# Output projection of a conformer-attention encoder: weights re-cut from four 256-column to two 512-column blocks, with a new, fully pinned order

## The chip, the cores and the metric

One NeuronCore of a Trainium2 chip. The core has five engines that run their own queues in order: PE (TensorE, matrix products into PSUM; its weight loads are shown as PEld), DVE (VectorE), ACT (ScalarE), POOL (GpSimd) and SP (SyncE, which issues the DMAs here). The metric is the device time of one execution in microseconds (us), as the median of several runs. Verdicts are about this time alone.

## What is computed

Two sequences of 512 tokens (a prompt and a sample), each with 16 meta tokens in front, go through one encoder layer. Width is 1024, everything is float32. Cut to what matters here:

```
hn = rms(h) ; z = hn @ w_in                       # gate, value, latent q, latent kv, rope key
u  = silu(layernorm(depthwise_conv(c_val * sigmoid(c_gate))))   # 512 channels
o  = attention(q, k, v)                           # 8 heads x 64 = 512 columns
h  = h + concat([u, o]) @ w_out                   # the output projection, 1024 x 1024
h  = h + (silu(rms(h) @ w_gate) * (rms(h) @ w_up)) @ w_down
return rms(h)[:, 16:]
```

The change concerns the line with `w_out`, the layer norm and silu of the convolution that feed it, and the order in which these stand beside the attention's end and the FFN's beginning.

## The kernel before

**Numbers.** Every product of float32 matrices is made of three matmuls in a reduced format: each operand is split into a high part (a cast, on ACT) and a low part (the remainder, a subtraction on DVE or POOL), and `mm3` (L160) multiplies high by high, high by low and low by high into the same PSUM place. A weight tile of 128 x 1024 floats is loaded and split by `pair` (L143): a DMA to a `raw` tile (two of them), a cast on ACT (L149), a subtraction on POOL (L152), into one of four `pair` tiles.

**PSUM.** There are four one-bank places (`bank`, tile `pt`) and two two-bank places (`bank2`, tile `ps`; the FFN's transposes use them as `px`).

**The output projection.** The K dimension of 1024 has two halves: half 0 is the convolution branch (`u`), half 1 the attention branch (`o`), each four tiles of 128 rows. The output's 1024 columns are cut in four blocks `dq` of 256, the tokens in eight tiles `t` of 128 (t = 0 to 3 the first sequence, 4 to 7 the second). `w_out_block(half, dq, t)` (L988) is 12 matmuls, each 128 tokens x 256 columns, and one DVE addition of the PSUM place onto the residual tile `hres[t]` (L994). `hres[0]` to `hres[2]` are tiles of their own; `hres[3]` to `hres[7]` lie in `slots`, where the attention had put its output `o`; x is loaded into them (L986) once that has been split. A weight tile `wo[2 * dq + half]` holds four k tiles by 256 columns.

**Half 1 and the layer norm.** Token tile 0 of half 1 is multiplied early, as a filler in the attention's last head (`early_blocks`, L864). The rest runs in the loop at L1006: `dq` from 0 to 3, `t` from 1 to 7, and at given positions (`steps`, numbered dq * 8 + t) stand the layer norm of a token tile (`layer_norm`, L946: four transposes into a two-bank place, statistics on DVE, two small POOL operations, one DVE operation, one ACT operation into one of two `xs` tiles), the way back (`layer_back`, L968: four transposes, one ACT copy into `U`) and the silu with its split (`conv_silu`, L975: two ACT operations, one DVE). The first layer norm stands at position 2, each further one 2 later, the way back 4 after it. After each `dq` the half-0 weight pair of that `dq` is loaded.

**Who sets the order.** Without more, the framework's planner orders the instructions of each engine by priority and its own time estimate. An instruction passed through `pin` (L125) while `pinned[0]` is true is kept behind everything that the program has issued to that engine before it. In the kernel before, `pinned[0]` becomes true only after the half-1 loop, at L1241, and the operations of layer norm, way back, silu and weight split aren't passed through `pin` at all.

**Half 0 and the FFN's beginning.** The list in `run` (L1276) is a hand-written order: tuples `(dq, t)` are half-0 blocks; `sq(t)` is the sum of squares of a finished token tile (ACT, then two POOL operations, L192 to L194; it also writes the tile to DRAM); `sc(t)` scales it (two DVE operations, L1045); `tu(t, s)` transposes eight 128 x 128 tiles on PE into a two-bank place (L1060); `do(t, stages)` splits tokens t and t + 4 and their sums and differences (the FFN uses Strassen-like combinations; L1064 to L1101); `co(j)` makes the weight operands of FFN unit 0 (L1136 to L1154), and the second list adds `pr(j)`, that unit's products over tokens 0 to 255.

## Time and profile before

| | |
|---|---|
| median of 3 runs | 1099.79 us (1099.77 to 1099.86) |
| the profiled execution | 1100.08 us; span of its instructions 1098.3 us |
| granted TensorE clock | 0.999 |
| DVE, ACT, POOL busy | 829.0, 497.5, 475.9 us |
| half-0 and half-1 matmuls of the projection from the loop's tiles | 128 x 256 |
| matmuls of the FFN | 128 x 512 for the most part |

The profile is one execution seen by the hardware profiler. A row of a timeline gives the start in us from the span's start, the duration, engine, line, operation, and output tile <- input tiles with shapes; a bracket at its end gives the idle time ahead of it and who ended it. A duration of a matmul is modelled and overlaps the next one's, so the distance between starts is what one costs. `x2` after a row means two instructions merged into it. A row of the windows gives, for each engine, the busy time inside the stretch and the number of instructions. The chain of waits is followed back from the last instruction: at each step to what released it.

### The profile page before, as it was taken

What the parts mean: (1) busy time and instruction counts of PE and PEld (TensorE: products, weight loads), DVE (VectorE), ACT (ScalarE), POOL (GpSimd) and SP (SyncE); (2) the same over time, 40 slices, a digit from 0 to 9 for tenths busy, and PEclk for the clock granted to TensorE, in tenths of its full rate; (3) what the DMA queues carried; (4) which work ended last, traced back from release to release, by engine and by line L of the source; (5) the groups of instructions that cost most, each with busy time, mean ns of one, the idle gap of its engine ahead of it and who ended that gap; (6) DMA issues with size and microseconds to landing.
All of it is one profiled execution on the core that took longest, in us unless ns stands there. A gap on an engine that the chain in (4) does not pass through costs nothing.

```text
span 1098.3 us, 16027 instructions
## 1 busy us (share of the span) xinstructions
PE 1075.8 (98%) x5922; PEld 929.5 (85%) x5922; DVE 829.0 (75%) x1206; ACT 497.5 (45%) x836; POOL 475.9 (43%) x419
## 2 busy tenths in 40 slices
PE   8999999999999999899999999999999999999997
PEld 8989888888888999788888888888888888888886
DVE  5699997888887646999877876877687496656643
ACT  6554525787786534542223233322322355433331
POOL 4689735564563233775544554554555200000012
PEclk9999999999999999999999999999999999999999
DMA  7211111110100412245445426444543899865503
GB/s 295 78 39 44 44 39 61 39 55 4 40 22 35 157 58 97 77 148 186 130 160 192 169 94 207 164 140 148 201 157 103 298 329 338 293 197 182 182 22 133
DMA packets 71422, 147.08 MB, mean 134 GB/s; under 512 B 6944, under 2 KB 29728, under 8 KB 71344
## 3 DMA queue, kind: packets, MB, share of 16 engines
q1 hardware_dynamic: 71344, 146.06, 38.9%
q8 instruction: 47, 0.77, 0.3%
q14 instruction: 31, 0.25, 0.1%
HBM read 105.92 MB, written 40.11 MB: 133 GB/s over the span
## 4 chain that ended last, share of the span: by engine, by line
PE 56%; DVE 2%; issue 2%; DMA 0%; POOL 0%; ACT 0%; POOLq 0%; ACTq 0%; SPq 0%; DVEq 0%
PE pt L167 48%; PE ps L167 8%; DMA raw<-in_w_gate_dram 0%; DVE tt L1045 0%; DVE hf L1045 0%; DVE tt L1136 0%; DVE slots L994 0%; DVE act_l L1067 0%; POOL rs L194 0%; DVE h L1087 0%; POOL slots L1442 0%; DVE slots L1086 0%; DVE slots L1094 0%; DVE a12l L1067 0%; DVE h L1091 0%
## 5 line engine op out<-in xcount | busy, mean ns | idle before, releaser
L167 PE MATMUL pt<-act_h,wc 128*128 128x512 f32 (+1 forms) x552 | 175.1, 380 | 0.0
L1154 POOL TENSOR_TENSOR wc<-tt,wc 128x512 fp32r<-128x512 f32 x88 | 124.6, 1432 | 104.4 <-ACT wc L1152 60.2
L167 PEld LDWEIGHTS pt<-act_h,wc 128*128 128x128 f32 x552 | 102.5, 188 | 19.6
L193 POOL TENSOR_SCALAR ms<-ms 128x1 f32<-128x1 f32 x15 | 7.3, 485 | 242.6 <-ACT re L192 214.1
L167 PE MATMUL pt<-hn_h,wp 128*128 128x512 f32 (+2 forms) x448 | 107.0, 331 | 0.0
L167 PE MATMUL pt<-act_l,wc 128*128 128x512 f32 (+1 forms) x276 | 104.8, 380 | 0.0
L1152 ACT CAST wc<-tt 128x512 fp32r<-128x512 f32 x88 | 51.4, 617 | 116.5 <-PE pt L167 109.8
L1334 DVE TENSOR_TENSOR re<-re,re 128x1024 fp32r<-128x1024 f32 x53 | 64.1, 1223 | 45.9 <-ACT re L1333 45.8
L1333 ACT CAST re<-re 128x1024 fp32r<-128x1024 f32 x53 | 55.0, 1054 | 69.2 <-PE ps L167 20.0
L167 PE MATMUL pt<-re 128*128 128x512 f32 x360 | 84.0, 389 | 0.0
L167 PEld LDWEIGHTS pt<-hn_h,wp 128*128 128x128 f32 x448 | 75.8, 188 | 8.5
L167 PEld LDWEIGHTS pt<-re 128*128 128x128 f32 x360 | 67.6, 188 | 14.0
L152 POOL TENSOR_TENSOR wp<-raw,wp 128x1024 fp32r<-128x1024 f32 x24 | 58.5, 2439 | 40.5 <-ACT wp L149 40.5
L167 PE MATMUL pt<-hn_l,wp 128*128 128x512 f32 (+2 forms) x224 | 74.5, 332 | 0.0
L742 POOL TENSOR_SCALAR p<-p,sst 128x512 f32<-128x512 f32 x64 | 44.1, 696 | 65.3 <-DVE sst L740 57.4
L167 PE MATMUL pt<-wp,act_h 128*128 128x256 f32 x384 | 71.2, 285 | 0.0
L1154 POOL TENSOR_TENSOR wc<-raw,wc 128x512 fp32r<-128x512 f32 x33 | 45.5, 1390 | 52.1 <-ACT wc L1152 52.1
L167 PE MATMUL ps<-re 128*128 128x512 f32 x276 | 63.9, 389 | 0.0
L367 POOL TENSOR_TENSOR pacc<-pacc,prod 128x512 f32<-128x512 f32 x43 | 58.3, 1355 | 7.0 <-ACT prod L365 4.3
L167 PEld LDWEIGHTS ps<-re 128*128 128x128 f32 x276 | 51.8, 188 | 10.7
L167 PEld LDWEIGHTS pt<-act_l,wc 128*128 128x128 f32 x276 | 51.9, 188 | 9.8
L167 PEld LDWEIGHTS pt<-wp,act_h 128*128 128x128 f32 x384 | 59.9, 192 | 0.2
(296 smaller groups left out, 2937.5 us busy)
## 6 DMA issues: line engine op xcount, KB each, us to landing
raw<-in_w_gate_dram SPq DMA_DIRECT2D x22, 512.0 KB, 3.9
hf<-in_w_down_dram SPq DMA_DIRECT2D x44, 256.0 KB, 4.8
re<-in_w_down_dram SPq DMA_DIRECT2D x31, 256.0 KB, 5.3
raw<-in_w_in_dram SPq DMA_DIRECT2D x12, 512.0 KB, 3.6
slots<-in_w_up_dram SPq DMA_DIRECT2D x11, 512.0 KB, 3.5
h<-in_w_up_dram SPq DMA_DIRECT2D x11, 512.0 KB, 5.5
d_t1t<-hf SPq DMA_DIRECT2D x22, 256.0 KB, 5.4
d_t4t<-hf SPq DMA_DIRECT2D x22, 256.0 KB, 2.5
```

What stands on the lines that cost most here:

```text
L152: nc.gpsimd.tensor_sub(lo[:, a], raw[:, a], hi[:, a].bitcast(F32))
L167: pin(nc.tensor.matmul(out_ap, lhsT=w_, rhs=m_, start=first and i + j == 0, stop=last and i == n - 1 and j == 2))
L193: pin(nc.gpsimd.tensor_scalar(ms[:rows], ms[:rows], EPS, 0.0, op0=ALU.add, op1=ALU.add))
L367: nc.gpsimd.tensor_add(acc, acc, to)
L742: nc.gpsimd.tensor_scalar(pr[:, real], pr[:, real], st[:, 2, t:t + 1], 1.0, op0=ALU.mult, op1=ALU.mult)
L1152: pin(nc.scalar.copy(w[:, 0:512], src))
L1154: pin(lo_eng.tensor_sub(w[:, 512:1024], src, w[:, 0:512].bitcast(F32)))
L1333: nc.scalar.copy(w[:, :, LO], blocks[n])
L1334: nc.vector.tensor_sub(w[:, :, HI], blocks[n], w[:, :, LO].bitcast(F32))
```

## The change

1. The projection's weights are packed as two k tiles by 512 columns per 128 x 1024 tile, eight tiles as before: `wo[4 * e + 2 * half + k // 2]` holds k tiles k and k + 1 of column half `e`. `wo_cut` picks a k tile's 512 columns.
2. `w_out_block(half, e, t)` makes 12 matmuls of 128 x 512 and one addition of 128 x 512. There are 16 half-0 blocks where there were 32, and 14 in the half-1 loop where there were 28. The early filler has as many steps (8), each of 3 matmuls of 512 columns in place of 6 of 256.
3. `pinned[0]` becomes true before the half-1 loop, and layer norm, way back, silu, the early addition and the casts and subtractions of `pair` are passed through `pin`. DMAs are not.
4. Positions: block (e, t) stands at e * 16 + 2 * t and is followed by the steps of that and the next position. Layer norm i stands at 6 + 2 * i, the way back at 10 + 2 * i, the silus of sequence s at 20 + 6 * s + c. Token tile 0 has no block in the loop, but its positions' steps stay.
5. The weight pairs of half 0's first column half (wo[0], wo[1]) are made after blocks (1, 4) and (1, 5) of the half-1 loop; those of the second (wo[4], wo[5]) inside the half-0 list (`ld`), as is the load of the first FFN weights.
6. The half-0 list has a new order.

```diff
@@ -49,7 +49,7 @@
 POOL_TAPS = (12, 13, 10, 12)
 LATE_TAPS = 0
 WARM = (36, 4, 8)
-LN_FIRST = 2
+LN_FIRST = 6
 LN_BACK = 4
 LN_STEP = 2
 SILU_STEP = 2
@@ -77,6 +77,7 @@
 ORDER_DOWN = (0, 1, 2, 4, 3, 6, 5)
 LOAD_AT = 5
 WO_AT = (4, 6)
+WO_CONV_AT = (4, 5)
 MM = "h"
 SC = "w"
 PV = False
@@ -146,10 +147,10 @@
         raw = raw_load(src)
         both = pool.tile([P, 2, 1024], F32R, tag=tag, bufs=bufs, name=name("wp"))
         hi, lo = both[:, 0, :], both[:, 1, :]
-        nc.scalar.copy(hi, raw)
+        pin(nc.scalar.copy(hi, raw))
         for a in range(0, 1024, LO_W):
             a = slice(a, a + LO_W)
-            nc.gpsimd.tensor_sub(lo[:, a], raw[:, a], hi[:, a].bitcast(F32))
+            pin(nc.gpsimd.tensor_sub(lo[:, a], raw[:, a], hi[:, a].bitcast(F32)))
         return hi, lo
 
     def split(hi, lo, src, pin=False):
@@ -861,18 +862,20 @@
         split(to[0][:, :, cs], to[1][:, :, cs], o[:, :, s * SEQ + t * 128:s * SEQ + (t + 1) * 128],
               pin)
 
+    def wo_cut(e, half, k):
+
+        return tuple(wx[:, k % 2 * 512:(k % 2 + 1) * 512] for wx in wo[4 * e + 2 * half + k // 2])
+
     def early_blocks():
 
         for t in range(EARLY):
-            for dq in range(4):
-                if dq == 0:
+            for e in range(2):
+                if e == 0:
                     early.append(bank2())
-                out_ap = early[t][:, dq // 2, dq % 2 * 256:(dq % 2 + 1) * 256]
                 cs = slice(t * 128, (t + 1) * 128)
-                for k0 in (0, 2):
-                    mm3(out_ap, [(o_first[0][:, k, cs], o_first[1][:, k, cs]) for k in (k0, k0 + 1)],
-                        [tuple(wx[:, k * 256:(k + 1) * 256] for wx in wo[2 * dq + 1]) for k in (k0, k0 + 1)],
-                        first=k0 == 0, last=k0 == 2)
+                for k in range(4):
+                    mm3(early[t][:, e, :], [(o_first[0][:, k, cs], o_first[1][:, k, cs])], [wo_cut(e, 1, k)],
+                        first=k == 0, last=k == 3)
                     yield
 
     filler = early_blocks()
@@ -880,7 +883,7 @@
         if s == 0 and h == LOAD_AT:
             wvp = load_attn(1)
         if s == 1 and h in WO_AT:
-            for n in (4 * WO_AT.index(h) + 1, 4 * WO_AT.index(h) + 3):
+            for n in (4 * WO_AT.index(h) + 2, 4 * WO_AT.index(h) + 3):
                 wo[n] = pair(w_out[n])
         nxt = heads[i + 1] if i + 1 < len(heads) else None
         if nxt is not None:
@@ -950,19 +953,19 @@
         pt = bank((P, 4, 128)) if LN_T else bank2()[:, 0].rearrange("p (c n) -> p c n", c=4)
         for c in range(NCH):
             src = late[:, s] if c == NCH - 1 else U[:, c, s]
-            nc.tensor.transpose(pt[:, c, :], src[:, ts], ident)
+            pin(nc.tensor.transpose(pt[:, c, :], src[:, ts], ident))
         st = const.tile([P, 6], F32, tag="bst", bufs=2, name=name("bst"))
         ag = const.tile([P, 2], F32, tag="bag", bufs=2, name=name("bag"))
         rs = const.tile([P, 1], F32, tag="brs", bufs=2, name=name("brs"))
         nm = const.tile([P, 1], F32, tag="bnm", bufs=2, name=name("bnm"))
         flat = pt.rearrange("p c n -> p (c n)")
-        nc.vector.bn_stats(st, flat)
-        nc.vector.bn_aggr(ag, st)
-        nc.gpsimd.tensor_scalar(rs, ag[:, 1:2], EPS, 0.0, op0=ALU.add, op1=ALU.add)
-        nc.gpsimd.tensor_tensor(rs, rs, mhalf[:, 0:1], op=ALU.pow)
-        nc.vector.scalar_tensor_tensor(nm, ag[:, 0:1], -1.0, rs, ALU.mult, ALU.mult)
+        pin(nc.vector.bn_stats(st, flat))
+        pin(nc.vector.bn_aggr(ag, st))
+        pin(nc.gpsimd.tensor_scalar(rs, ag[:, 1:2], EPS, 0.0, op0=ALU.add, op1=ALU.add))
+        pin(nc.gpsimd.tensor_tensor(rs, rs, mhalf[:, 0:1], op=ALU.pow))
+        pin(nc.vector.scalar_tensor_tensor(nm, ag[:, 0:1], -1.0, rs, ALU.mult, ALU.mult))
         xs = normed[i] = lnp.tile([P, SEQ], F32, tag="xs", bufs=XS, name=name("xs"))
-        nc.scalar.activation(xs, flat, AF.Identity, scale=rs, bias=nm)
+        pin(nc.scalar.activation(xs, flat, AF.Identity, scale=rs, bias=nm))
 
     def layer_back(i):
         s, t = divmod(i, 4)
@@ -970,28 +973,27 @@
         xs = normed[i]
         pt = bank((P, 4, 128)) if LB_T else bank2()[:, 0].rearrange("p (c n) -> p c n", c=4)
         for c in range(NCH):
-            nc.tensor.transpose(pt[:, c, :], xs[:, c * 128:(c + 1) * 128], ident)
-        nc.scalar.copy(U[:, :, s, ts], pt)
+            pin(nc.tensor.transpose(pt[:, c, :], xs[:, c * 128:(c + 1) * 128], ident))
+        pin(nc.scalar.copy(U[:, :, s, ts], pt))
 
     def conv_silu(c, s):
         u = U[:, c, s, 0:SEQ]
-        nc.scalar.activation(u, u, AF.Silu, scale=ln_g[:, c:c + 1], bias=ln_b[:, c:c + 1])
+        pin(nc.scalar.activation(u, u, AF.Silu, scale=ln_g[:, c:c + 1], bias=ln_b[:, c:c + 1]))
         hi, lo = act[0][s][0][:, c], act[0][s][1][:, c]
-        nc.scalar.copy(hi, u)
-        nc.vector.tensor_sub(lo, u, hi.bitcast(F32))
+        pin(nc.scalar.copy(hi, u))
+        pin(nc.vector.tensor_sub(lo, u, hi.bitcast(F32)))
 
     for t in range(4):
         split_o(act[1][1], 1, t)
     for t in range(8):
         nc.sync.dma_start(hres[t], x[t * 128:(t + 1) * 128, :])
 
-    def w_out_block(half, dq, t):
-        s, cs, ds = t // 4, slice(t % 4 * 128, t % 4 * 128 + 128), slice(dq * 256, (dq + 1) * 256)
+    def w_out_block(half, e, t):
+        s, cs, ds = t // 4, slice(t % 4 * 128, t % 4 * 128 + 128), slice(e * 512, (e + 1) * 512)
         pt = bank()
-        w = wo[2 * dq + half]
-        mm3(pt[:, :256], [(act[half][s][0][:, k, cs], act[half][s][1][:, k, cs]) for k in range(4)],
-            [tuple(wx[:, k * 256:(k + 1) * 256] for wx in w) for k in range(4)])
-        pin(nc.vector.tensor_add(hres[t][:, ds], pt[:, :256], hres[t][:, ds]))
+        mm3(pt, [(act[half][s][0][:, k, cs], act[half][s][1][:, k, cs]) for k in range(4)],
+            [wo_cut(e, half, k) for k in range(4)])
+        pin(nc.vector.tensor_add(hres[t][:, ds], pt, hres[t][:, ds]))
 
 
     steps = {}
@@ -1000,19 +1002,25 @@
         steps.setdefault(LN_FIRST + LN_STEP * i + LN_BACK, []).append((layer_back, (i,)))
     for s in range(NSEQ):
         for c in range(NCH):
-            at = LN_FIRST + LN_STEP * (4 * s + 3) + LN_BACK + 1 + SILU_STEP * c
+            at = 20 + 6 * s + c
             steps.setdefault(at, []).append((conv_silu, (c, s)))
     assert not late_left
-    for dq in range(4):
+
+    pinned[0] = True
+    for e in range(2):
         for t in range(8):
+            at = e * 16 + 2 * t
             if t >= EARLY:
-                w_out_block(1, dq, t)
-            if dq * 8 + t >= EARLY_AT and early:
+                w_out_block(1, e, t)
+            if at >= EARLY_AT and early:
                 i = EARLY - len(early)
-                nc.vector.tensor_add(hres[i], early.pop(0).rearrange("p a b -> p (a b)"), hres[i])
-            for f, a in steps.pop(dq * 8 + t, ()):
-                f(*a)
-        wo[2 * dq] = pair(w_out[2 * dq])
+                pin(nc.vector.tensor_add(hres[i], early.pop(0).rearrange("p a b -> p (a b)"), hres[i]))
+            for a_ in (at, at + 1):
+                for f, a in steps.pop(a_, ()):
+                    f(*a)
+            if e and t in WO_CONV_AT:
+                n = WO_CONV_AT.index(t)
+                wo[n] = pair(w_out[n])
     assert not steps
     ln_pool.__exit__(None, None, None)
     cqkv_pool.__exit__(None, None, None)
@@ -1237,9 +1245,6 @@
             for t in ts:
                 w_out_block(0, dq, t)
 
-
-    pinned[0] = True
-
     def run(steps):
 
         for step in steps:
@@ -1272,15 +1277,18 @@
     def do(t, stages):
         return lambda: turns[t].do(stages)
 
-    units[0].load()
-    run([(0, 0), (1, 0), (2, 0), (0, 4), (1, 4), (2, 4), (3, 0), sq(0), (3, 4), sq(4),
-         (0, 1), (1, 1), sc(0), (2, 1), sc(4), (3, 1), sq(1), tu(0, 0), do(0, "a"), (0, 5), tu(0, 1), do(0, "A"), do(0, "b"),
-         (1, 5), do(0, "ce"), (2, 5), do(0, "d"), (3, 5), sq(5), do(0, "x"),
-         (0, 2), sc(1), (1, 2), sc(5), do(0, "y"), (2, 2), (3, 2), sq(2), tu(1, 0), do(1, "a"), (0, 6), tu(1, 1), do(1, "A"),
-         do(1, "b"), (1, 6), do(1, "ce"), (2, 6), do(1, "d"), (3, 6), sq(6),
-         (0, 3), sc(2), do(1, "x"), (0, 7), sc(6), co(0), do(1, "y"), (1, 3), tu(2, 0), do(2, "a"), co(1), (1, 7),
-         tu(2, 1), do(2, "A"), do(2, "b"), co(2), (2, 3), co(3), do(2, "ce"), (2, 7), do(2, "d"), co(4), (3, 3), sq(3),
-         co(5), (3, 7), sq(7), co(6)])
+    def ld(n):
+        def load():
+            wo[n] = pair(w_out[n])
+        return load
+
+    run([(0, 0), ld(4), (0, 4), ld(5), (0, 1), units[0].load, (1, 0), sq(0), (1, 4), sq(4), (1, 1), sq(1), sc(0),
+         (0, 5), sc(4), tu(0, 0), do(0, "a"), sc(1), (1, 5), sq(5), tu(0, 1), do(0, "A"), do(0, "b"), do(0, "ce"),
+         (0, 2), sc(5), do(0, "d"), do(0, "x"), tu(1, 0), do(1, "a"), (0, 6), do(0, "y"), tu(1, 1), do(1, "A"),
+         do(1, "b"), (1, 2), sq(2), do(1, "ce"), (1, 6), sq(6), do(1, "d"),
+         (0, 3), sc(2), do(1, "x"), (0, 7), sc(6), co(0), do(1, "y"), tu(2, 0), do(2, "a"), co(1),
+         tu(2, 1), do(2, "A"), do(2, "b"), co(2), co(3), (1, 3), sq(3), do(2, "ce"), do(2, "d"), co(4),
+         co(5), (1, 7), sq(7), co(6)])
 
     run([pr(0), sc(3), pr(1), sc(7), pr(2), do(2, "xy"), units[1].load, pr(3), tu(3, 0), do(3, "a"), pr(4), do(3, "b"),
          tu(3, 1), do(3, "A"), pr(5), do(3, "ce"), pr(6), do(3, "x")])
@@ -1508,7 +1516,7 @@
     kv = a["w_kv_up"][0].reshape(LORA, H, DN + DV)
     wk = _pack(kv[:, :, :DN].reshape(LORA, H * DN), KL, H * DN)[0]
     wv = _pack(kv[:, :, DN:].reshape(LORA, H * DV), KL, H * DV)[0]
-    w_out = _pack(a["w_out"][0], KD, 256).reshape(4, 128, 2, 1024).transpose(0, 2, 1, 3).reshape(8, 128, 1024)
+    w_out = _pack(a["w_out"][0], KD, 512).reshape(2, 128, 4, 1024).transpose(0, 2, 1, 3).reshape(8, 128, 1024)
     w_gate = _pack(a["w_gate"][0], KD, 128)
     w_up = _pack(a["w_up"][0], KD, 128)
     w_down = a["w_down"][0].reshape(NFF, 128, D)
```

## The prediction

> **What bounds the kernel now.** I read the page's busy table first, then the chain of waits, then the timelines of the projection, about 354 to 469 us.
>
> ```profile
> PE 1075.8 (98%) x5922; PEld 929.5 (85%) x5922; DVE 829.0 (75%) x1206; ACT 497.5 (45%) x836; POOL 475.9 (43%) x419
> ```
>
> PE looks like the bound everywhere. The chain that ended last says otherwise for the place that the change touches:
>
> ```profile
> 465.00 3.46 DVE tt L1045 x2
> 468.46 0.04 issue
> 468.50 0.66 PE px L1060 x4
> 469.16 12.95 PE pt L167 x108
> ```
>
> From 469.16 on, the chain is matmuls: whoever delays that point delays the end by as much. What sets it is the last FFN scaling on DVE (L1045). So the projection has two parts. In the first (half 1, layer norm) PE is nearly the bound. In the second (half 0 and the hand-over to the first FFN products) a DVE/ACT/POOL chain ends last, and a faster matmul is not passed on by itself. I forecast the shift of 468.50, the start of the last four transposes.
>
> **The wider matmuls.** PE rows, narrow matmuls and transposes first, then 512-wide ones from a later stage:
>
> ```profile
> 353.90 0.40 PE L167 MATMUL pt<-wp,cq_h 128*128 128x256 f32 x2
> ...
> 388.82 0.28 PE L167 MATMUL pt<-wp,act_h 128*128 128x256 f32 x1
> ...
> 389.79 0.49 PE L953 MATMUL ps<-ident,U 128*128 128x128 f32 x3
> ...
> 419.16 1.03 PE L1060 MATMUL px<-ident,hf 128*128 128x128 f32 x8
> 419.95 0.36 PE L167 MATMUL pt<-wp,act_h 128*128 128x256 f32 x1
> ...
> 559.72 0.39 PE L167 MATMUL pt<-act_l,wc 128*128 128x512 f32 x1
> ...
> 560.86 0.39 PE L167 MATMUL pt<-a12h,wc 128*128 128x512 f32 x1
> ```
>
> From 388.82 to 389.79 eight narrow matmuls start: 0.121 us each. From 559.72 to 560.86 five wide ones: 0.228 us each. The projection is 4 x 8 x 2 x 4 x 3 = 768 narrow ones, 92.9 us; it becomes 384 wide ones, 87.6 us. PE saves 5.4 us: 0.3 in the early block, 2.4 in half 1, 2.7 in half 0. Eight transposes cost 0.79 (419.16 to 419.95), four about 0.36.
>
> [...]
>
> **Half 1, before.** It starts at 353.90. Before the transposes at 419.16 stand twelve blocks of half 0 (12 x 12 x 0.121 = 17.4), so half 0 starts at 401.7: 47.8 us, of which 28 x 1.45 = 40.6 are blocks.
>
> **Half 1, after.** Every instruction is now pinned behind its predecessor. Layer norm 0's four transposes leave the end of attention, and the early block is 0.3 shorter, so I take 353.5 as the start (bounds 353.1 and 353.9). Fourteen blocks of 12 x 0.228 = 2.74 make 38.3; sixteen groups of transposes, mostly in pairs, 6.1. Without waits half 0 would start at 397.9. Three waits are added.
>
> First, the adds of tokens 3 to 7 need x in the place of attention's output, and layer norm now stands behind add 3 on DVE. Before:
>
> ```profile
> 357.89 1.23 DVE L1012 TENSOR_TENSOR h<-ps,h 128x1024 f32<-128x1024 f32 x1 [0.52 <-DMA h<-in_x_dram]
> ```
> ```profile
> 361.54 2.24 SPq L986 DMA_DIRECT2D slots<-in_x_dram  x5
> ```
> ```profile
> 364.87 0.42 DVE L994 TENSOR_TENSOR slots<-pt,slots 128x256 f32<-128x256 f32 x1 [0.49 <-DMA slots<-in_x_dram]
> ```
>
> The load waited for the last splits, in front of which the planner had put the early add and a layer-norm statistic. Both now come after them: the load starts about 2 us earlier, at 359.5, and lands 3.3 later (364.87 - 361.54), at 362.8. Layer norm 0 starts on DVE at 363 instead of 362; its result is wanted at 368. Cost nothing; if the load stays where it was, 0.5 to 2.
>
> Second, the layer-norm chain, which has only two wide PSUM places:
>
> ```profile
> 390.42 0.70 DVE L959 BATCH_NORM_STATS2 bst<-ps 128x6 f32<-128x512 f32 x1 [0.60 <-PE ps L953]
> 391.15 0.18 DVE L960 BATCH_NORM_AGGREGATE bag<-bst 128x2 f32<-128x6 f32 x1
> ...
> 392.40 0.16 DVE L963 SCALAR_TENSOR_TENSOR bnm<-bag,brs 128x1 f32<-128x1 f32 x1 [0.40 <-POOL brs L962]
> ```
> ```profile
> 392.88 0.79 ACT L965 ACTIVATE xs<-ps,bnm,brs 128x512 f32<-128x512 f32 x1
> ```
>
> From the transposes at 389.79 to nm's end at 392.56 is 2.77; with ACT's 0.79 the place is free after 3.6. PE comes back to it after a block and eight transposes, 2.74 + 0.79 = 3.53: a wait of about 0.1 each time, six times. But between layer norm 4 and 5 no block stands (the loop skips token 0 in both column halves), so only back 3 covers it: 3.6 - 0.79 leaves a stall of about 2.3 (the copies' own latency is in it). All following on PE is pinned and can't fill it. So half 0 starts at 397.9 + 0.6 + 2.3 = 400.8.
>
> Third, the start of half 0 itself. ACT from layer norm 7 on:
>
> ```profile
> 376.13 0.59 ACT L974 COPY U<-ps 128x512 f32<-128x512 f32 x1 [1.93 <-PE ps L973]
> 376.74 1.28 ACT L978 ACT_TABLE_LOAD   x1
> 378.03 2.93 ACT L978 ACTIVATE U<-U,sm 128x512 f32<-128x512 f32 x4
> ```
> ```profile
> 400.27 2.17 ACT L980 CAST act_h<-U 128x512 fp32r<-128x512 f32 x4
> 402.34 1.04 ACT L149 CAST wp<-raw 128x1024 fp32r<-128x1024 f32 x1
> ```
> ```profile
> 403.46 2.61 POOL L152 TENSOR_TENSOR wp<-raw,wp 128x1024 fp32r<-128x1024 f32 x1 [7.99 <-ACT wp L149]
> ```
>
> Layer norm 7's transposes start five blocks, two lone groups and themselves before half 0: 400.8 - 13.7 - 1.1 = 386.0, its result is there at 389.6. Then ACT, in its pinned order, must do the table load 1.28, two back copies 1.0, six silu-and-cast pairs of about 1.36 (a cast waits for its silu; in batches they took 1.28) and two weight casts of 1.0 before wo[1]'s high half is done: 389.6 + 1.3 + 1.0 + 8.2 + 2.0 = 402.1. POOL's low half, 2.6: 404.7. The first block of half 0 wants it at its eighth matmul, 400.8 + 7 x 0.228 = 402.4: a stall of 2.3. Behind it on ACT are the last two silus and the casts of wo[4] and wo[5]; PE wants those only 3 blocks later, by which time they are done. Half 0 is thus as if started at 403.1, against 401.7: half 1 as a whole loses 1.4 in spite of 2.4 saved. The bounds of this stall are 0 (each silu and its cast back to back, as in the batches, and layer norm 7 earlier) and 3.7 (another 1.4 on ACT, about a table load more).
>
> [...]
>
> **Half 0 and the hand-over.** Before: 401.7 to 468.50, 66.8. After: thirteen blocks up to (0,3), 35.6, four turns, 3.2, and two waits of turn 1, for a PSUM place behind DVE's three subtractions (0.7) and for the second place behind the slowed scaling of token 5 (1.2): (0,3) ends at 443.8. From there DVE is never idle, as in the present kernel. Its prices, alone and beside a POOL subtraction:
>
> ```profile
> 428.72 1.41 DVE L1045 SCALAR_TENSOR_TENSOR tt<-h,rs,gain 128x512 f32<-128x512 f32 x2
> ```
> ```profile
> 430.89 3.46 DVE L1045 SCALAR_TENSOR_TENSOR tt<-slots,rs,gain 128x512 f32<-128x512 f32 x2 [0.43 <-POOL rs L194]
> ```
> ```profile
> 452.10 1.66 DVE L1136 TENSOR_TENSOR tt<-raw,tt 128x512 f32<-128x512 f32 x1
> 453.69 0.41 DVE L994 TENSOR_TENSOR slots<-pt,slots 128x256 f32<-128x256 f32 x1
> 454.02 1.45 DVE L1136 TENSOR_TENSOR tt<-raw 128x512 f32<-128x512 f32 x1
> ```
>
> After 443.8 + 0.2: add 0.6 (a 512-wide PSUM read, as 390.42); scale 2, slowed, 3.46; add 0.6; scale 6, slowed, 3.46; two lows 1.2; three weight differences 2.3 (1.8 alone, some 4.2 slowed: POOL has a gap just there, so nearer the first); add 0.6; five subtractions of turn 2, 3.3; t4 and the last add 1.3: 460.8. Then the square and the POOL queue:
>
> ```profile
> 461.08 1.05 ACT L192 ACTIVATE s4l<-slots 128x1024 fp32r<-128x1024 f32 x1
> ```
> ```profile
> 464.05 0.92 POOL L194 TENSOR_TENSOR rs<-ms,tiny 128x1 f32<-128x1 f32 x1
> ```
>
> Square 7 started at 461.08 and its scale came at 464.97, 3.9 later; taken over, 460.8 + 3.9 = 464.7, and scale 7, slowed, 3.46: 468.2. Against 468.46 that is 0.3 earlier. Sums of this length miss small gaps, so I take 0.3 as it is: 1100.08 of the profiled execution becomes 1099.8; the runs' median, 1099.79, lies 0.3 under that execution, so I predict 1099.5.
>
> **Rivals.** (1) The two stalls of half 1 don't come: the PSUM place is freed sooner, or wo[1] is ready in time. Half 0 then starts 4.6 earlier (2.3 + 2.3), and the hand-over shifts with it, since everything in it hangs on that start: 1094.9. For it: ACT is only 57% busy from 354 to 402 by its rows' sum (27.45 of 48), so there is room if the order were less strict. Against: the order is strict, and the chain from layer norm 7 to wo[1] has no gap to squeeze.
>
> ```profile
> 354.00:402.00 48.00, 47.33 (x398) 46.84 (x397) 27.45 (x62) 27.45 (x42) 12.72 (x17) 1.00 0.34 121
> ```
>
> (2) Slower: DVE meets POOL more often in the hand-over. Each scaling or difference that falls beside a POOL subtraction costs 1.0 more (1.73 against 0.70). My sum leaves the three differences and scale 3 mostly free; if these five are caught, 468.2 becomes 473: up to 1104. It decides against the kernel from three more caught operations on (1102.5). For it: in the present trace two of three differences are caught. Against: the POOL work between them is the same, only elsewhere.
>
> (3) PE is the bound after all, and all 5.4 arrive with the stalls of before kept: 1094.4. The chain above 468.50 speaks against it.
>
> **How the numbers follow.** A run of this kernel can be told from no change at about 0.2%, 2.2 us. My forecast and its near neighbours (each single term at its bound: the start +-0.4, the load +2, the boundary -2.3 or +1.4, differences +1.9) have 0.50, and lie mostly inside 2.2 us. Rival 1, whole or in the larger half, 0.24; rival 3, 0.05; rival 2, 0.21. Faster by over 0.2%: 0.29; within: 0.50; slower: 0.21. The range leaves out the last tenth of each side: 1095.0 to 1102.8; the forecast's own, 1097.3 to 1102.
>
> **What would show it.** Right: 512-wide matmuls at 0.228; a PE gap of about 2 us ahead of layer norm 5's transposes; another inside the first block of half 0, put down to POOL wp (L152); DVE full from about 444 to 468; the last transposes of turn 3 within 2 us of 468.5. Wrong: PE without gaps at those two places (rival 1), or many 1.7 us scalings and differences at 444 to 470 and turn 3 after 471 (rival 2).

## The result and the profile after

| | before | after |
|---|---|---|
| median of 6 runs, us | 1099.82 (1099.5 to 1100.64) | 1106.78 (1104.2 to 1108.42) |
| ratio, 95% interval | | 1.0059 (1.0048 to 1.007) |
| profiled execution, us | 1100.08 | 1108.15 |
| its span, us | 1098.3 | 1106.3 |
| start of the last four transposes of turn 3, us | 468.50 | 476.87 |

The kernel is slower by 7 us, and the time lies above the whole range. The point that the forecast followed moved by 8.4 us and the span by 8.0: all of the loss stands ahead of that point. The runs of the changed kernel differ by 4.2 us among themselves, those of the kernel before by 1.1.

In the busy table after, TensorE has 384 instructions fewer and yet 2 us more of busy time:

```profile
PE 1078.1 (97%) x5538; PEld 912.7 (82%) x5538; DVE 829.2 (75%) x1176; ACT 498.5 (45%) x836; POOL 473.3 (43%) x419
```

The windows of the same execution say why. The column behind the five busy times, PEclk, is the clock that TensorE was granted, as a share of its full rate:

```profile
core 0: us, PE busy (x) PEld busy (x) DVE busy (x) ACT busy (x) POOL busy (x), PEclk, DMA share, GB/s
...
354.00:381.00 27.00, 24.14 (x121) 19.39 (x120) 15.36 (x30) 8.30 (x15) 3.99 (x10) 1.00 0.44 156
381.00:386.00 5.00, 4.85 (x17) 3.87 (x18) 1.04 (x3) 1.35 (x3) 0.79 (x2) 0.66 0.00 0
386.00:409.00 23.00, 21.14 (x105) 17.27 (x104) 12.15 (x19) 17.62 (x26) 6.35 (x6) 1.00 0.08 24
409.00:413.00 4.00, 4.00 (x11) 3.13 (x12) 2.21 (x4) 1.72 (x3) 2.38 (x1) 0.57 0.41 131
413.00:453.00 40.00, 37.46 (x181) 30.83 (x180) 25.14 (x35) 17.07 (x32) 14.30 (x19) 1.00 0.28 106
453.00:476.00 23.00, 20.15 (x116) 17.20 (x114) 20.71 (x23) 12.68 (x25) 17.70 (x15) 0.85 0.23 72
```

Three windows have a clock under 1. In the kernel before, the same windows all have 1.00. 5 x 0.34, 4 x 0.43 and 23 x 0.15 make 1.7, 1.7 and 3.5 us of clock that are missing, 6.9 in all. The clock's own record has it at half rate for 3.4 us from 381.8, for 3.4 from 409.1 and for 6.8 from 456.9. Each begins at or soon after a wait of TensorE, as its timeline shows (in brackets: the idle time ahead and what ended it):

```profile
381.15 0.55 PE L956 MATMUL ps<-ident,U 128*128 128x128 f32 x3 [2.34 <-ACT xs L968]
...
408.82 0.60 PE L168 MATMUL pt<-wp,act_h 128*128 128x512 f32 x1 [1.86 <-POOL wp L153]
409.21 0.63 PE L168 MATMUL pt<-wp,act_l 128*128 128x512 f32 x1
409.64 1.05 PE L168 MATMUL pt<-wp,act_h 128*128 128x512 f32 x2
410.49 0.63 PE L168 MATMUL pt<-wp,act_l 128*128 128x512 f32 x1
410.92 1.05 PE L168 MATMUL pt<-wp,act_h 128*128 128x512 f32 x2
```
```profile
437.05 1.07 PE L1068 MATMUL px<-ident,tt 128*128 128x128 f32 x8 [1.63 <-DVE h L1099]
441.78 1.06 PE L1068 MATMUL px<-ident,tt 128*128 128x128 f32 x8 [0.91 <-DVE act_l L1075]
453.61 0.60 PE L1068 MATMUL px<-ident,hf 128*128 128x128 f32 x4
454.91 0.66 PE L1068 MATMUL px<-ident,hf 128*128 128x128 f32 x4 [0.70 <-DVE hf L1053]
456.68 0.93 PE L1068 MATMUL px<-ident,hf 128*128 128x128 f32 x4 [1.11 <-DVE hf L1053]
458.26 1.12 PE L1068 MATMUL px<-ident,hf 128*128 128x128 f32 x4 [0.66 <-DVE hf L1053]
```

The first row is the wait ahead of layer norm 5, the second that inside half 0's first block; both had been forecast. From 409.64 to 410.92 three wide matmuls start, 0.427 us each, where at full clock it is 0.227. The last four rows are turn 2, whose two halves now stand one behind the other with no block between them: three waits in 5 us.

The end of the chain of waits after:

```profile
473.36 3.46 DVE tt L1053 x2
476.82 0.04 issue
476.87 0.66 PE px L1068 x4
477.53 2.51 PE pt L168 x21
```

It has the same form as before: the scaling of token 7 (now L1053), the last transposes, and then matmuls to the end. Only it comes 8.4 us later.

### The profile page after: what moved, and what is told of

Same layout as the page of the kernel before. It is cut to its first block, busy times and chain, and to the rows that moved or that the text cites. A ratio compares the mean times of both kernels' runs of the same rounds, so it can differ in the third digit from the quotient of the medians.

```text
span 1106.3 us, 15243 instructions
## 1 busy us (share of the span) xinstructions
PE 1078.1 (97%) x5538; PEld 912.7 (82%) x5538; DVE 829.2 (75%) x1176; ACT 498.5 (45%) x836; POOL 473.3 (43%) x419
## 4 chain that ended last, share of the span: by engine, by line
PE 81%; DVE 11%; ACT 4%; issue 2%; DMA 1%; POOL 1%; SPq 0%; POOLq 0%; ACTq 0%; DVEq 0%
PE pt L168 58%; PE ps L168 13%; PE pt L798 3%; PE pt L768 2%; PE pt L299 2%; DVE ps L390 2%; DVE ps L398 2%; DVE pacc L400 1%; PE px L278 1%; PE pt L589 1%; ACT p L740 1%; DMA h<-in_x_dram 1%; DVE tt L1053 1%; DMA gain<-in_gains_dram 1%; DVE hf L1053 0%
## 5 line engine op out<-in xcount | busy, mean ns | idle before, releaser
L168 PE MATMUL pt<-wp,act_h 128*128 128x512 f32 x192 | 63.4, 411 | 1.9 <-POOL wp L153 1.9
L168 PE MATMUL pt<-s1h,wc 128*128 128x512 f32 (+1 forms) x184 | 58.4, 380 | 0.0
```

The source lines that it names most:

```text
L168: pin(nc.tensor.matmul(out_ap, lhsT=w_, rhs=m_, start=first and i + j == 0, stop=last and i == n - 1 and j == 2))
```

## The experiments

The theory at first: TensorE's waits are longer than the sum had them, and after the longest of them its clock is halved for a while, so that they are paid for once more. Rivals: the waits alone, or the clock alone; VectorE's chain of half 0 fixes turn 3 whatever happens ahead of it; the order as such costs nothing, or the wide tiles bring nothing. The letters A, B and C in the expectations are defined anew in each of them. Times are medians, the brackets hold the ratio to the kernel before in the same series and its 95% interval; that kernel took 1099.8 to 1099.9 us each time.

### Spare work in the gaps: fill_three and fill_two

```diff
+    def fill(w, n):
+        pt = bank()
+        for i in range(n):
+            pin(nc.tensor.matmul(pt, lhsT=w[:, 0:128], rhs=w[:, 0:512], start=i == 0, stop=i == n - 1))
...
+                    if f is layer_norm and a == (5,):
+                        fill(wo[6][0], 10)
...
+                if self.t == 2 and (k == 4 or k == 0 and s):
+                    fill(wo[4][0], 5)
...
+    fill(wo[0][0], 9)
     run([(0, 0), ld(4), (0, 4), ld(5), (0, 1), units[0].load, (1, 0), sq(0), (1, 4), sq(4), (1, 1), sq(1), sc(0),
```

fill_two is without the lines in turn 2.

> The changed kernel with spare matmuls (their result is read by nobody) where PE has none for several us: 10 ahead of layer norm 5's transposes, 9 ahead of half 0's first block, and three times 5 between and inside the two transposes of FFN turn 2. The clock theory (PE's idle stretches let the granted clock fall to a half, and the slow matmuls after them are what the change costs): the three half-clock stretches go, granted clock 0.999, the time falls by the 6.8 us that they cost in the profiled execution, to about 1101.5, and the runs lie as close together as the kernel before's. The wait theory (the time is lost in the waits themselves, PE at half clock only does more slowly what it would wait for anyway): the waits stay, so 1104 to 1108 as the changed kernel.

> As the former, but with the spare matmuls at the first two places only (layer norm 5, first block of half 0). The clock theory: the two half-clock stretches of 3.4 us at 381 and 409 us go, 3.4 us in all, the one at turn 2 stays: about 1103.5, granted clock 0.995 to 0.997. The wait theory: 1104 to 1108.

fill_three took 1104.67 us (ratio 1.0044, 1.0031 to 1.0056), fill_two 1105.5 (1.0053, 1.004 to 1.0066). Windows of fill_three:

```profile
381.00:413.00 32.00, 31.98 (x154) 25.83 (x152) 16.02 (x26) 21.46 (x30) 10.15 (x10) 1.00 0.12 36
...
453.00:476.00 23.00, 21.27 (x146) 19.08 (x145) 22.36 (x28) 14.31 (x28) 19.56 (x17) 1.00 0.40 133
```

The clock stays at 1.00 where TensorE has spare work; in fill_two only the stretch of turn 2, which it leaves empty, was left (a clock of 0.66 from 452 to 462, which is 6.8 us at half rate). Turn 3's last transposes come at 472.55 in fill_three, 4.3 of the 8.4 us earlier. The other 4.05 remain with no clock lost: the clock alone is refuted, and its 1101.5 us was missed. By the time alone both kernels lie in the range of the wait theory; it is the windows that show the clock's part. This part may be somewhat larger than 4.3, because the spare work overruns its gap: half 1 ends at 404.18 in fill_three, against 405.20 less 1.7 of clock in the changed kernel, 0.7 later (an estimate). In the median run, whose mean clock is higher, the part is smaller.

### Back to the planner for half 1: late_pin

The pinning begins behind half 1's loop instead of ahead of it:

```diff
-    pinned[0] = True
     for e in range(2):
         for t in range(8):
...
+    pinned[0] = True
+
     def run(steps):
```

> The changed kernel with the pinning begun after half 1 again, as in the kernel before, so that the planner orders half 1, layer norm and silu with 512-column blocks; half 0's list stays. The wait theory: the stalls at layer norm 5 (2.6 us) and in half 0's first block (2.0 us) go, the rest stays: 1102 or so. The clock theory: with the stalls both half-clock stretches go too, 4.6 + 3.4 us, and the one at turn 2 stays: 1098 to 1100. A third theory, that the new half-0 list is what costs: 1104 or more.

1108.33 us (1.0073, 1.006 to 1.0085). The places of the layer norms were made for the written order. Left to the planner, the last of them come so late that half 0 waits for its operands, and the clock is 0.68 from 400 to 416, which is 10.2 us at half rate:

```profile
404.05 1.07 PE L976 MATMUL ps<-ident,xs 128*128 128x128 f32 x4 [1.72 <-ACT xs L968]
...
410.69 1.22 PE L168 MATMUL pt<-wp,act_h 128*128 128x512 f32 x2 [4.14 <-ACT act_h L983]
```

So pinning is not what made the changed kernel slow at these places; without it they are worse. What the wait theory and the clock theory expected was missed. The time lies where the third theory, a costly half-0 list, had it, but the waits shown stand ahead of that list and in its first block, so this run does not test it.

### A block between the halves of turn 2: block_between_turns

```diff
-         tu(2, 1), do(2, "A"), do(2, "b"), co(2), co(3), (1, 3), sq(3), do(2, "ce"), do(2, "d"), co(4),
+         (1, 3), sq(3), tu(2, 1), do(2, "A"), do(2, "b"), co(2), co(3), do(2, "ce"), do(2, "d"), co(4),
```

> The changed kernel with block (1, 3) and its square put between the two transposes of FFN turn 2, in place of behind them, so that PE has a block of 2.7 us in the stretch of 5.4 us without matmuls. The clock theory: the half-clock stretch at turn 2, 6.8 us long in the profiled execution and worth 3.4, goes: about 1103.5, clock 0.995 to 0.997. The wait theory: DVE ends the hand-over, and a block moved on PE changes under 1 us: 1106.

1105.72 us (1.0046, 1.0032 to 1.0059). The window 450 to 470 has the clock at 1.00 and turn 2 loses two of its three waits; the stretch near 408 is still there (0.83 from 404 to 414), and none follows layer norm 5's wait in this execution (1.00 from 376 to 386). Turn 3's last transposes: 473.1. The median is the wait theory's (1106); the gain of 0.1 to 1.1 us, by which series of the changed kernel it is compared with, does not stand out from the spread of the runs.

### The layer norms' PSUM places: ln_on_t

The norms' transposes go into the ring of four places that the projection's blocks use, instead of sharing two with the transposes back:

```diff
-LN_T = False
+LN_T = True
```

> The changed kernel (1106.8 us) with the layer norms' transposes written into the ring of four PSUM places that the projection's blocks use, so that they no longer share two places with the transposes back. Theory A (the missing microseconds begin in half 1: two places tie each layer norm to the end of the one before it, 3.75 us a step, and the skipped block before layer norm 5 leaves 2.6 us on TensorE, after which its clock halves for 3.4 us): the waits of half 1 (0.8, 0.3 and 2.6 us) go, the half-rate stretch near 382 goes, and the time falls by 3.7 to 5.4 us, to 1101.4 to 1103.1. Theory B (what is lost is lost behind turn 1, in VectorE's chain, whatever half 1 does): half 1 ends earlier, the last transposes of turn 3 do not move with it, 1106 to 1107. Theory C (the order on VectorE, ScalarE and GpSimd, not the PSUM places, ties the norms): the wait before layer norm 5 stays above 1.5 us.

1101.26 us (1.0017, 1.0007 to 1.0027), the largest gain of a single edit. The wait ahead of layer norm 5 is gone and the clock is full there; the wait for the weights stays, with its stretch:

```profile
404.76 0.50 PE L168 MATMUL pt<-wp,act_h 128*128 128x512 f32 x1 [1.86 <-POOL wp L153]
```
```profile
376.00:386.00 10.00, 10.00 (x59) 8.60 (x58) 4.51 (x13) 4.30 (x7) 3.15 (x8) 1.00 0.01 2
402.00:412.00 10.00, 8.13 (x29) 6.21 (x29) 4.99 (x7) 4.93 (x7) 7.13 (x3) 0.83 0.46 157
```

The time is 0.1 us below theory A's range. Theory C is out, since the wait did not stay. So the two places tied each norm to the one before it, and turn 3 moved with half 1 (473.1): VectorE's chain does not hold it. The eleven runs fall into two groups: six at 1099.93 to 1101.26 with a mean clock of 0.997, five at 1103.05 to 1104.32 with 0.992 or 0.993. The two groups of one and the same program lie 3.9 us apart, and the clock goes with them. The profiled execution is of the slower group; no trace shows the other.

### The weights earlier: wo_early

```diff
-WO_CONV_AT = (4, 5)
+WO_CONV_AT = (2, 3)
```

> The changed kernel with the weights of the first two half-0 tiles made two steps earlier (after the third and fourth token of the second 512 columns instead of the fifth and sixth). Theory A (each wait on TensorE is passed on to turn 3, and is paid again by the clock): the 2.0 us inside the first half-0 block go, the stretch at half rate near 409 goes with them, together 3.7 us: 1103.1, last transposes of turn 3 near 473.2. Theory B (turn 3 hangs on VectorE's chain, which starts elsewhere): 1106 to 1107, and the 2 us come back as waits in turns 0 to 2. If the earlier casts hold up the silus of the second sequence instead, the second half-0 block waits for the last of them: up to 1 us of the gain is lost.

1104.85 us (1.0044, 1.0032 to 1.0056). The wait inside the first block is gone, and 404 to 414 has a clock of 1.00. In the profiled execution, whose mean clock is 0.994, layer norm 0 comes 3 us late, at 365.33; from there to the last transposes of turn 3 it takes 107.9 us against 114.6. Layer norm 5 waits 2.33 us, and in this execution no stretch follows (1.00 from 380 to 390). The time lies between the two theories' ranges, so the rows alone speak for theory A here.

### Square 5 later: sq5_later

```diff
-         (0, 5), sc(4), tu(0, 0), do(0, "a"), sc(1), (1, 5), sq(5), tu(0, 1), do(0, "A"), do(0, "b"), do(0, "ce"),
+         (0, 5), sc(4), tu(0, 0), do(0, "a"), sc(1), (1, 5), tu(0, 1), do(0, "A"), do(0, "b"), sq(5), do(0, "ce"),
```

> The changed kernel with the square of token tile 5 put behind the copy and the split of turn 0 on ScalarE's queue, instead of ahead of them. Theory A (TensorE's wait of 1.8 us before turn 1, forecast at 0.7, comes from the square standing ahead of the copies that VectorE waits for, 1.03 us): the wait falls by about 1 us, and the time by 0.5 to 1.1: 1105.7 to 1106.3. Theory B: VectorE's scaling of tile 5 then waits as much longer for the square, and the time stays, 1106.8.

1105.04 us (1.0042, 1.0029 to 1.0055). The wait ahead of turn 1 is 0.9 us shorter, and the scaling of token 5 does not come later for it:

```profile
435.30 1.06 PE L1068 MATMUL px<-ident,tt 128*128 128x128 f32 x8 [0.70 <-DVE h L1099]
```

The row is as theory A had it. The time is below both ranges, and beside the spread of the runs it proves little.

### All four: four_edits

> The changed kernel with all of it at once: layer norms in the ring of four, weights two steps earlier, square 5 later, and the block (1, 3) with square 3 between the two halves of turn 2. Theory A (waits add up and each is passed on): 3.7 to 5.4 from half 1, 3.7 from the boundary, 0.5 to 1.1 from turn 1 and 1.1 from turn 2, 9 to 11 us in all but no more than until VectorE's chain of half 0 is the bound, 1096 to 1099, with no stretch at half rate but that behind the last matmuls; the projection's wide tiles would then gain 1 to 4 us on the kernel before. Theory B: VectorE's chain of half 0 holds turn 3 where it is, 1103 to 1106, even though no stretch at half rate is left.

1096.56 us (1096.01 to 1097.75), ratio 0.9972 (0.9961 to 0.9984): faster than both kernels. Its busy table, and the windows in which the changed kernel lost its time:

```profile
PE 1071.2 (98%) x5538; PEld 907.8 (83%) x5538; DVE 826.8 (75%) x1176; ACT 499.2 (46%) x836; POOL 473.6 (43%) x419
```
```profile
381.00:386.00 5.00, 5.00 (x31) 4.30 (x30) 2.41 (x7) 2.82 (x6) 1.57 (x4) 1.00 0.02 3
386.00:409.00 23.00, 23.00 (x108) 19.06 (x107) 11.74 (x19) 18.29 (x25) 8.79 (x6) 1.00 0.13 46
409.00:413.00 4.00, 4.00 (x18) 3.01 (x17) 1.38 (x2) 0.11 (x1) 1.59 (x1) 1.00 0.66 223
...
453.00:476.00 23.00, 19.68 (x160) 18.81 (x159) 22.31 (x34) 14.44 (x29) 15.10 (x13) 1.00 0.47 161
```

From 381 to 413 TensorE is never idle, and no window has a clock under 1. Theory A is borne out, in time and windows, and theory B, VectorE's chain as a fixed end, is refuted. The gain on the changed kernel is 9.1 us if its series of 1105.76 (after_again, below) is taken, and 10.2 if that of 1106.78 is, each by its distance from the kernel before. The four edits one by one brought 4.4 (norms), 0.8 (weights), 0.6 (square) and 0.1 (turn 2), 5.9 together, by the first series, and 5.5, 1.9, 1.7 and 1.1, 10.2 together, by the second. Whether together they are worth more than their sum is therefore open.

### The tiles by themselves: after_again, narrow_new_order, narrow_four_edits

```diff
-        mm3(pt, [(act[half][s][0][:, k, cs], act[half][s][1][:, k, cs]) for k in range(4)],
-            [wo_cut(e, half, k) for k in range(4)])
+        for c in (slice(0, 256), slice(256, 512)):
+            mm3(pt[:, c], [(act[half][s][0][:, k, cs], act[half][s][1][:, k, cs]) for k in range(4)],
+                [tuple(w[:, c] for w in wo_cut(e, half, k)) for k in range(4)])
```

This keeps order, tiles and adds and makes each matmul 256 wide again, in the changed kernel (narrow_new_order) and in the one with four edits. after_again is the changed kernel, unaltered.

> The changed kernel itself beside the three that follow: 1104 to 1108, with two to four stretches at half rate, not always the same ones. It is the measure of what the next kernels change.

> The changed kernel with its order and its tiles of weights, but each projection block of the two halves as two runs of 12 matmuls of 256 columns instead of 12 of 512. Per block that is 24 x 0.121 instead of 12 x 0.2267, 0.18 us more, 5.6 us over the 31 blocks that are changed (the early one keeps its form). Theory A (the tiles gain what was forecast and the order loses more): where the chain of the layer norms sets the pace, 3.75 us a step, TensorE's 3.7 with narrow blocks hides beneath it, about 1.5 us; the rest comes through, so 2.5 to 4.5 us slower than the changed kernel. Theory B (all that the wide tiles save was hidden behind waits): the same time as the changed kernel within 1 us.

> The kernel with the four edits (1096.6 us), with its blocks as two runs of 256 columns. Nothing of half 1 waits there, so its 15 blocks of 0.18 us come through in full, 2.7 us; of half 0's 16 blocks (2.9 us) those come through that stand ahead of the place where VectorE sets the pace. Theory A: 3.5 to 5.6 us slower, 1100.1 to 1102.2, so no faster than the kernel before: the gain of the four edits is that of the wide tiles, let through. Theory B (the gain is the new order's own): 1096.6 to 1098.

1105.76 (1103.99 to 1108.5), 1107.74 (1105.56 to 1109.07) and 1098.71 us (1098.52 to 1099.55). The wide matmuls save TensorE 5.5 us here: 14 blocks in half 1 and 16 in half 0 at 0.18 each, 30 and not the 31 of the expectation. Of these, 2.0 reach the end in the changed kernel, within its spread, and 2.15 in the one with four edits, where the runs don't overlap. Both are under what theory A expected. With narrow matmuls the kernel with four edits is still faster than the kernel before (0.9989, 0.9981 to 0.9998). So the other 1.2 us of its gain come from what it keeps, the order with the new tiles and the fewer, wider additions, which these runs don't tell apart. In half 0 the transposes of turn 1 and turn 3 wait for VectorE with either width, and part of what TensorE saves ends in these waits.

### What keeps the clock up: fill_transposes

fill_two with transposes in place of the spare matmuls:

```diff
-        for i in range(n):
-            pin(nc.tensor.matmul(pt, lhsT=w[:, 0:128], rhs=w[:, 0:512], start=i == 0, stop=i == n - 1))
+        for i in range(2 * n):
+            pin(nc.tensor.transpose(pt[:, i % 4 * 128:(i % 4 + 1) * 128], ident, ident))
```

> The kernel with spare work in two places (10 matmuls of 512 columns ahead of layer norm 5, 9 ahead of half 0's first block; the stretches near 382 and 409 were gone), with 20 and 18 transposes of 128 columns in place of the matmuls, about the same time on TensorE. Theory A (only ordinary matmuls keep the clock up): stretches of 3.4 us at half rate again near 382 to 385 and 408 to 411, and 1105.5 to 1109. Theory B (any work does, the idle time is what counts): no stretch but that near 455, and 1103.6 to 1106.5, as with the matmuls.

1104.54 us (1.0044, 1.003 to 1.0057):

```profile
378.66 2.35 PE L1002 MATMUL pt<-ident 128*128 128x128 f32 x20
```
```profile
378.00:388.00 10.00, 9.73 (x61) 8.24 (x61) 3.82 (x10) 2.86 (x6) 2.36 (x6) 1.00 0.01 2
```

No stretch at either place (from 404 to 414 the clock is 1.00 too), only one near 455 as in fill_two (0.83 from 452 to 462): theory B. Here 2.35 us of transposes kept the clock up as matmuls did. That alone would not prove it, because with the gap left empty layer norm 5's wait of 2.3 us was followed by a stretch in the profiled executions of the changed kernel and of sq5_later (0.66 from 381 to 386 and 0.72 from 380 to 386), but not in those of block_between_turns and wo_early (1.00). But from 377.06 to 381.59 TensorE ran transposes and no matmul, and the clock stayed full. In block_between_turns it was 0.16 us of matmuls, 1.66 of transposes and 1.59 of idle time from 376.94 to 380.35, with the same result.

### The old kernel pinned: pin_alone, pin_alone_2, pin_alone_on_t

The kernel before with `pin(...)` around the instructions that the change wraps, and with the pinning from half 1's loop on; old tiles, old places for the norms. The third has `LN_T = True` too.

```diff
+    pinned[0] = True
     for dq in range(4):
         for t in range(8):
...
-    pinned[0] = True
```

> The kernel before, with its blocks of 256 columns, its tiles of weights and its places for the layer norms, but with all of half 1 pinned to the order of the code. Theory A (written order ties the norms to each other by their two places, and the skipped blocks of token 0 leave TensorE without projection work): a step of two narrow blocks and eight transposes is 3.7 us beside a chain of 3.75, so few waits but those at the skipped blocks (steps 8 and 16), 1 to 2 us each, and a stretch at half rate when one is over 2 us: 1101 to 1105. Theory B (pinning by itself costs nothing; the loss comes from the new places and blocks): 1099.5 to 1100.5.

> The kernel before with half 1 pinned to the order of the code, once more, for its profile: 1114.8 to 1118.0 as in the three undisturbed executions. Theory A (two PSUM places tie the norms): the steps of the norms are 3.75 us or more with TensorE waiting for ScalarE's xs at each, 5 us or more in all in half 1. Theory C (the weights' casts and subtractions, pinned at the end of each 256 columns, stand ahead of the norms' and silus' work on ScalarE and GpSimd): the waits are at the ends of the columns and at the boundary, over 3 us each, and the norms keep under 4 us a step.

> The same with the norms' transposes in the ring of four places. Theory A: most of the 17 us go, 1101 to 1106. Theory C: 1113 to 1117.

pin_alone's profiled execution took 2763.78 us, with slow matmuls all through and no record of the clock (TensorE busy 2752.6 us), and is left out; its three others took 1114.82 to 1117.99 us. pin_alone_2 took 1116.2 (1.0148, 1.013 to 1.0167), pin_alone_on_t 1113.58 (1.0125, 1.0111 to 1.0138). TensorE and VectorE of pin_alone_2:

```profile
366.11 0.90 PE L953 MATMUL ps<-ident,U 128*128 128x128 f32 x3 [5.46 <-ACT xs L965]
...
395.15 0.90 PE L953 MATMUL ps<-ident,U 128*128 128x128 f32 x3 [2.84 <-ACT xs L965]
```
```profile
361.50 0.42 DVE L994 TENSOR_TENSOR h<-pt,h 128x256 f32<-128x256 f32 x1 [1.50 <-DMA h<-in_x_dram]
362.75 0.42 DVE L994 TENSOR_TENSOR h<-pt,h 128x256 f32<-128x256 f32 x1 [0.82 <-DMA h<-in_x_dram]
363.09 0.69 DVE L959 BATCH_NORM_STATS2 bst<-ps 128x6 f32<-128x512 f32 x1
```

and TensorE and VectorE of pin_alone_on_t:

```profile
375.89 0.60 PE L167 MATMUL pt<-wp,cq_h 128*128 128x256 f32 x2 [1.92 <-DVE h L994]
...
397.49 0.80 PE L167 MATMUL pt<-wp,act_h 128*128 128x256 f32 x2 [3.19 <-DVE h L994]
```
```profile
375.35 0.16 DVE L963 SCALAR_TENSOR_TENSOR bnm<-bag,brs 128x1 f32<-128x1 f32 x1 [4.08 <-POOL brs L962]
375.42 0.75 DVE L994 TENSOR_TENSOR h<-pt,h 128x256 f32<-128x256 f32 x2
```

With the norms in their old places, written order sets layer norm 0's statistics behind two adds that wait for x: TensorE stands for 5.5 us, and the clock is 0.66 from 362 to 372, which is 6.8 us at half rate. The two places in PSUM (theory A) explain 2.6 of the 16 us. With four places the blocks wait for VectorE's adds, these for a norm's small step, and that for GpSimd, which has the weights' subtraction (2.4 us, started at 372.0) in front of the norm's power: theory C, seen at 375 and once more at 394, but at 1.9 and 3.2 us of TensorE's time and not over 3 each. So no single theory holds, and each place was read from the rows and not tried by itself. Both expectations for pin_alone were missed, by 10 us and more. What follows is that pinning alone is by far the worst version. That the later places for the norms and the weights' steps make it bearable is likely, but no run moves them alone.

## Why the prediction was wrong

Marks of the profiled execution, forecast and measured. The forecast for layer norm 5 is worked out from the prediction's terms, the others stand in it. The last column is what is added from one mark to the next:

| | forecast | measured | difference | new here |
|---|---|---|---|---|
| half 1 starts | 353.5 | 354.1 | 0.6 | 0.6 |
| layer norm 5's transposes | 379.1 | 381.15 | 2.1 | 1.5 |
| layer norm 7's transposes | 386.0 | 390.1 | 4.1 | 2.0 |
| half 0 starts | 400.8 | 405.2 | 4.4 | 0.3 |
| (0, 3) ends | 443.8 | 450.8 | 7.0 | 2.6 |
| turn 3's last scaling ends | 468.2 | 476.8 | 8.6 | 1.6 |

**The wider matmuls: right.** They cost 0.227 us a piece. What reaches the end is 2 us of 5.5.

**The places of the stalls: right.** Ahead of layer norm 5 the row has 2.34 us against 2.3, inside half 0's first block 1.86, or 2.0 counted from start to start, against 2.3, put down to POOL wp as named. As written, 3.6 - 0.79 is 2.8; the 2.3 that was taken has no working, so its closeness is in part luck. The 1.4 us more on ScalarE, the upper bound at the boundary, is shown by no run: in the changed kernel the table load took 1.28 us, from 393.85, and the first silu stands right behind it, at 395.15. Rival 1 is out, and so is rival 3.

**What a stall costs: the step that failed.** "3.6 - 0.79 leaves a stall of about 2.3" and "a stall of 2.3" priced each at its idle time. Each was followed by 3.4 us at half rate, 1.7 us more: these are 1.7 of the 2.0 us from layer norm 5 to 7 and 1.7 of the 2.6 us in front of (0, 3). The third place, turn 2, was not seen as a stall at all, since VectorE was to be the bound there. There the clock was at half rate for 6.8 us, and the block (1, 3) ended so late that VectorE waited for it:

```profile
464.22 0.69 DVE L996 TENSOR_TENSOR slots<-pt,slots 128x512 f32<-128x512 f32 x1 [1.76 <-PE pt L168]
```

So the sign "DVE full from about 444 to 468" was wrong, and this is the 1.6 us of the last line. In fill_three, whose clock is full, the same addition starts at 459.90 without a wait. Clock in all: 1.7 + 1.7 + 1.6 = 5.0 of 8.6 us by these marks; fill_three gives 4.3, and 5.0 with the 0.7 by which its spare work is late. No rival held this. The profile of before could not show it either: its clock is at 1.00 from 343 to 500.

**Half 1's other waits: mis-sized.** The load of x into the places of attention's output was issued at 359.3 as forecast, but "cost nothing" overlooked the two adds in front, whose own x came late:

```profile
359.95 0.69 DVE L996 TENSOR_TENSOR h<-pt,h 128x512 f32<-128x512 f32 x1 [0.71 <-DMA h<-in_x_dram]
361.76 0.69 DVE L996 TENSOR_TENSOR h<-pt,h 128x512 f32<-128x512 f32 x1 [1.12 <-DMA h<-in_x_dram]
...
364.10 0.69 DVE L962 BATCH_NORM_STATS2 bst<-ps 128x6 f32<-128x512 f32 x1
```

Layer norm 0 came on VectorE at 364.1 instead of 363, and the third norm's transposes waited 0.8 (from start to start; 0.56 by the row). Then each step took 3.75 us, not 3.6. With the start that is 2.1 us up to layer norm 5. ln_on_t showed what ties these steps: the two PSUM places.

**Turn 1: mis-sized.** Its two waits were forecast at 0.7 + 1.2 and came to 1.8 + 1.1, counted from start to start (1.63 and 0.91 in the rows). Ahead of the first, VectorE itself waited for ScalarE, where square 5 stood ahead:

```profile
434.76 0.69 DVE L1094 TENSOR_TENSOR slots<-h,px 128x512 f32<-128x512 f32 x1 [1.03 <-ACT act_h L1072]
```

The forecast had walked VectorE's queue there and not ScalarE's; sq5_later takes 0.9 us of it away.

**Rival 2** had the sign right and the mechanism not. Scaling 3 did meet GpSimd (3.32 us for two operations), and so did one of the three differences (1.80 us), but square 7's way through GpSimd covered it, since scaling 7 still had to wait; turn 3 "after 471" came from TensorE's waits and its clock.

```profile
469.27 3.32 DVE L1053 SCALAR_TENSOR_TENSOR tt<-slots,rs,gain 128x512 f32<-128x512 f32 x2
...
473.36 3.45 DVE L1053 SCALAR_TENSOR_TENSOR tt<-slots,rs,gain 128x512 f32<-128x512 f32 x2 [0.43 <-POOL rs L195]
```

Clock-free, the waits add up to 0.6 + 1.5 + 0.3 + 0.3 + 1.0 - 0.3 = 3.4 us more than forecast, against 4.35 in fill_three (4.05 and the 0.3 of gain that was forecast). Of the 1 us between them, 0.7 is likely the spare work's own delay; 0.3 is not placed.

## What to carry to other kernels

When an order is written out by hand, walk every queue that it fixes, and look for the ring of buffers with two places that ties one step to the next: here a ring of four for the norms was worth 4.4 us or more, and the change's wider matmuls 2. A wait of TensorE of about 2 us can cost nearly twice its length: here 2.34 and 1.86 us of it were each followed by 3.4 us at half rate, 1.7 us more. So put a block of work between two dependent groups of transposes, and look at the granted clock before anything else is compared. A saving on an engine that is 98% busy is worth only what the waits behind it let through: 2 of 5.5 us.

## What the runs showed of the hardware

**Half rate came in pieces of 3.4 us, behind waits of about 2 us.** In the profiled execution of the changed kernel the clock's record changes at 381.76, 385.18, 409.07, 412.48, 456.86 and 463.68: two stretches of 3.41 us at half rate and one of 6.83. These edges lie whole multiples of 3.413 us apart; from 385.18 to 409.07, for one, it is 7 times 3.413.

Cut at these edges, and in steps of 3.413 us between them, 340.80 to 477.34 us of that execution gives 40 pieces, 36 of them at full rate. Three of the 36 had TensorE idle for 2.34, 1.86 and 1.81 us, and the piece behind each ran at half rate. Behind the other 33, with 1.25 us at most, the clock stayed full. Of the four pieces at half rate, one had 0.66 us of idle time and was followed by another; the three with none were followed by the full clock. In the kernel before, 40 pieces cut in the same way, from the change of its clock at 1095.13, have 1.49 us of idle time at most, and the clock is 1.00 in all of them.

Here idle time is what the windows leave beside PE busy, and transposes count as work. Counted as idle, they would spoil this: from 446.60 to 450.01 of the kernel before, matmuls kept TensorE busy for 0.88 us, and the clock stayed full; from 405.66 to 409.07 of the changed kernel it was 1.55 us, without a transpose, and half rate followed.

One and the same wait brought a stretch in one execution and not in another. This is layer norm 5's wait in the changed kernel and in block_between_turns:

```profile
378.35:381.76 3.41, 1.07 (x9) 0.83 (x8) 0.77 (x3) 1.25 (x2) 0.79 (x2) 1.00 0.00 0
381.76:385.18 3.42, 3.42 (x10) 2.64 (x9) 1.04 (x3) 0.78 (x1) 0.79 (x2) 0.50 0.00 0
```
```profile
376.94:380.35 3.41, 1.82 (x13) 1.20 (x11) 1.73 (x4) 1.04 (x2) 0.79 (x2) 1.00 0.00 0
380.35:383.76 3.41, 2.55 (x13) 2.19 (x14) 0.88 (x2) 1.25 (x2) 0.70 (x2) 1.00 0.00 0
```

In the first the whole wait lies in one piece, 2.34 us idle, and half rate follows. In the second it is spread over two, with 1.59 and 0.86 us, and the clock stays full. That the cut through the wait makes the difference is the author's reading of these two executions. The figures are those of this part of the program alone.

**A program's time went with its clock.** The 12 runs of the changed kernel go from 1103.99 us at a mean clock of 0.997 to 1108.5 at 0.992, with nothing else changed.
